# Leaving softmax probabilities undivided: inverse row sums moved into the output gates of both attention branches

## The chip, the cores and the metric

The kernel runs on one core of a Trainium2 chip. The core has a matrix engine (TensorE, PE in the profile), a vector engine (VectorE, DVE), a scalar engine (ScalarE, ACT), a general engine (GpSimd, POOL) and a queue that issues most transfers (SyncE, SP). The metric is the device time of one execution in microseconds (us); the median over the runs shown is what a change is judged by.

## The reference

Two layers of a Griffin-style block over 512 grid tokens (a grid of 8 rows by 64 columns) and 16 meta tokens, width 1024. Each layer makes one combined projection and splits it between grouped-query attention (branch A: 8 query heads, 2 key heads, head size 64) and neighbourhood attention on the grid (branch B: 8 heads, a clamped window of 8 by 16 neighbours and the meta keys). Each branch's output is multiplied by a SiLU gate, projected, merged by sigmoid gates and projected again.

```python
def attend(qb):                                   # branch A, also for the meta queries
    s = jnp.einsum('bqkgd,bskd->bkgqs', qb, k).astype(jnp.float32) * scale
    p = jax.nn.softmax(s, axis=-1).astype(v.dtype)
    return jnp.einsum('bkgqs,bskd->bqkgd', p, v)
...
# branch B, one grid row of queries
s = jnp.concatenate([s_win.reshape(b, NA_HEADS, GRID_W, kh * NA_KW), s_meta], axis=-1)
p = jax.nn.softmax(s, axis=-1).astype(v.dtype)
...
oa = gqa_attention(qa, ka, va) * jax.nn.silu(za)
ob = neighbourhood_attention(qb, kb, vb, rpb) * jax.nn.silu(zb)
ya = jnp.einsum('ble,ed->bld', oa, w_o_attn)
yb = jnp.einsum('ble,ed->bld', ob, w_o_na)
mixed = jax.nn.sigmoid(ga) * ya + jax.nn.sigmoid(gb) * yb
return x + jnp.einsum('bld,de->ble', mixed, w_out)
```

The inputs are drawn so that the scores are large (gains of the norms and of the bias table are scaled by about 8), so the row maximum is subtracted before the exponential.

## The kernel before, in words

**Layout.** Activations lie with features on the 128 partitions and the 528 tokens along the free axis, so a tile "512 or 528 wide" is one group of 128 features (a *pair* of heads, 64 partitions each) for all tokens. Everything is 32-bit. To keep accuracy, each operand of a big product is split into a rounded part (hi) and its remainder (lo) by `split` (L191: a cast on ACT at L193, a subtraction on DVE at L194), and a product is three matmuls (L325 to L327). Weights come in halves of 256 KB through four raw buffers; `weights` (L231) issues the load on SP (L235), casts on ACT (L240) and subtracts on POOL (L241), about one product ahead.

**Order of the work.** PE's backbone is the sequence of products: per layer 58 weight chunks, minus those of the last layer that are handled at the end. Each product covers the tokens in one span (second layer, 512 wide) or two (first layer, 264 wide each); 24 matmuls per span. After each span, and half way through a span of 512, `tick` (L310) lets the two attention branches emit one step. A unit of branch A starts every fourth tick and a head of branch B every fourth tick, one tick later; their further steps come a fixed number of ticks after their start, by the tables `GQA_AT` and `NA_AT` (L37 to L40). When the projections are over, `finish` (L299) lets the remaining ticks follow. What is emitted first has priority; a planner then orders each engine's instructions by priority and by the times that it expects, and the engines run their lists in that fixed order. `tc.high_priority()` lifts a piece; `tc.issue_after` holds one behind another on its engine.

**Branch A, one unit** (`global_unit`, L818; one head, two blocks of 128 queries, queries on partitions, 528 keys wide). `scores` at two ticks: `softmax` (L803) takes the scores from PSUM with the row maximum in one DVE operation (L810), negates the maximum (L813), applies the exponential on ACT with the row sum as a by-product (L814), then takes the inverse of the sum (L815) and multiplies the row by it (L816), both on DVE. `turn` (L833) transposes 32 by 32 blocks on DVE (L838) and, for the second block, writes the result to DRAM on SP (L841); `back` (L843) reads it so that keys lie on partitions (four transfers, L848, and a small one for the last keys, L851); `split_part` and `split_ends` make hi and lo parts (L193, L194, L867, L869); `sums` (L872) are the matmuls with the values (L876), in two groups of four and five. At the end `unit_done` (L903) adds the two halves of the result (`combine`, L765: a copy on ACT, an addition on DVE) into the pair's output tile; after the fourth unit of a pair `gated` (L775) multiplies that tile by the pair's gate on DVE (L777) and splits it. In the first layer there is also one unit per key head for the meta queries.

**Branch B, one head** (`windowed_head`, L931; four blocks of 128 queries against 208 or 272 keys). `prepare` loads the bias table; `scores` adds bias and takes the row extreme on DVE (L955), applies the exponential on ACT with row sums (L957), then inverts the sums (L953, L961, on DVE) and multiplies: two blocks on DVE (L960), two on ACT (L963). `transposes1` to `transposes3` turn the blocks on PE through two PSUM banks that they share with other small products and split them; `sums` multiplies with the values (L1022) and, for the second head of a pair, calls `gated` with the pair's gate `zb`. In the first layer the meta queries have their own small softmax (L971 to L974).

**Gates.** `silu_gate` (L752) makes `zb[j]` and `zgate[j]`, 128 partitions by 512 or 528 tokens, from the projections of pair j.

**The ends of the stages.** The products of branch B's output (WOB, written y<-ob in the profile) begin after the fourth of eight merge gates, which come behind the last pair's projection; those of branch A (WOA, y<-oa) follow in the same way behind a second set of eight merge gates. They take weight halves of four pieces, one piece per pair, so the last pair's gated tile is the fourth operand of the first of them.

The functions that the diff touches, with their callers:

Of the kernel before, what the change touches and what calls it, by code (L numbers as in the profile page):

```python
# [11 lines left out]
F32 = mybir.dt.float32  # L12
# [24 lines left out]
GQA_AT = ({"scores": (0, 2), "turn": (1, 3), "back": 4, "split": (5, 5), "ends": 5, "sums": (6, 7)},  # L37
          {"scores": (0, 1), "turn": (1, 2), "back": 3, "split": (5, 5), "ends": 5, "sums": (6, 7)})
# [57 lines left out]
def trunk_kernel(ctx: ExitStack, tc: tile.TileContext, xT, w, gn, gf, bias, rope, out):  # L96
# [357 lines left out]
    for l in range(DEPTH):  # L454
# [344 lines left out]


        zgate, oa, o_t, newest = {}, [None] * 4, {}, {}

        def softmax(p, q, qs, kv, k0, n, scale, name):  # L803
# [4 lines left out]
            with tc.high_priority():  # L808
# [5 lines left out]
                nc.scalar.activation(p[:n], p[:n], AF.Exp, bias=st[:n, 1:2], scale=1.0, accum_out=st[:n, 2:3])  # L814
            nc.vector.reciprocal(st[:n, 3:4], st[:n, 2:3])  # L815
            nc.vector.tensor_scalar_mul(p[:n], p[:n], st[:n, 3:4])  # L816

        def global_unit(kv, parts, n, name, done):  # L818
# [7 lines left out]
            def scores(i):  # L826
                q, qs, scale = parts[i]
# [3 lines left out]
                softmax(c["p"][i], q, qs, kv, NMETA - first_token[i], n, scale, f"{name}_{i}")  # L831
# [79 lines left out]
        def start_meta(kv):  # L911
            for j in (2 * kv, 2 * kv + 1):
                if j not in o_t:
                    o_t[j] = slot("T", f"oa{l}_{j}")
            return global_unit(kv, [(Q2m[kv], slice(0, 64), eighth)], 64, f"m{l}_{kv}", lambda av: meta_done(kv, av))

        def start_unit(hd, i):
            parts = [(Q2[hd], slice(P * t, P * (t + 1)), st["r8"][:, t, hd:hd + 1]) for t in (2 * i, 2 * i + 1)]
            return global_unit(hd // 4, parts, P, f"{l}_{hd}_{i}", lambda av: unit_done(hd, i, av))
# [11 lines left out]
        def windowed_head(hd):  # L931
# [9 lines left out]
            def scores():  # L941
                S = ps_s.tile([P, 2, 512], F32, tag="S", name=f"Sb{nm}")
                st = tiny.tile([P, 3, 4], F32, tag="stb", bufs=3, name=f"stb{nm}")
# [6 lines left out]
                for b, (base, k0, n) in enumerate(BLK):  # L950
                    i, c0 = BLK_PS[b]
                    if b == 2:
                        nc.vector.reciprocal(st[:, 2, :2], st[:, 1, :2])  # L953
                    with tc.high_priority():
                        nc.vector.tensor_tensor_reduce(pb[b], S[:, i, c0:c0 + n], pb[b], -1.0, 3e38,  # L955
                                                       ALU.add, ALU.min, st[:, 0, b:b + 1])
                    nc.scalar.activation(pb[b], pb[b], AF.Exp, bias=st[:, 0, b:b + 1], scale=-1.0,  # L957
                                         accum_out=st[:, 1, b:b + 1])
                for b in range(2):
                    nc.vector.tensor_scalar_mul(pb[b], pb[b], st[:, 2, b:b + 1])  # L960
# [320 lines left out]
```

## Time and profile before

| what | us |
|---|---|
| median of 3 runs (lowest, highest) | 867.78 (867.03, 868.68) |
| the profiled execution, its own time | 865.97 |
| its span, first to last instruction | 864.2 |
| time outside the span | 1.77 |
| PE busy in the span | 827.5 |
| DVE busy | 591.3 |
| ACT busy | 489.1 |
| POOL busy | 354.3 |

How to read it: "busy" counts an engine's instructions; an engine that waits for another is idle. Groups of instructions are named by the line of the kernel, the engine, the tile written, an arrow and the tiles read, followed by the shape, the count, and after a bar the busy time of the group, the mean duration of one in ns, and the idle time of the engine just before them with what ended it. "A <- B: t, n, longest" in the lists of waits says that instruction A of an engine waited for B, t us in total, n times. SPq stands for the queue of SP. DMA issues are listed with the KB of one and the median us from issue to landing. A table of windows gives, for a stretch of the span, the busy time of each engine and its instruction count.

### The profile page before, as it was taken

The page shows a single profiled execution, that of the slowest core. Times are in us where ns is not written, and L with a number is a line of the kernel's source. Part 1 is how long each engine was busy: PE and PEld are TensorE (multiplying, and loading weights), DVE is VectorE, ACT ScalarE, POOL GpSimd, SP SyncE. Part 2 cuts the span into 40 slices and gives each one's busy share as a digit, 9 for nine tenths or more (in the row PEclk, how much of TensorE's full clock was granted, in tenths as well). Part 3 has the DMA queues.
Part 4 walks back from the last instruction along what each step waited for, and adds up shares of the span by engine and source line. Part 5 has one row for each costly group of instructions (what it writes and reads, how often), then busy time and mean ns, then how long its engine had stood idle before and what let it go on. Part 6 is the DMA issues. An engine that isn't in the chain of part 4 may idle for free. (4 is left out here: it accounts for less than half of the span.)

```text
span 864.2 us, 16032 instructions
## 1 busy us (share of the span) xinstructions
PE 827.5 (96%) x5662; PEld 758.5 (88%) x5662; DVE 591.3 (68%) x1378; ACT 489.1 (57%) x1169; POOL 354.3 (41%) x279
## 2 busy tenths in 40 slices
PE   9999898989889999899999999999999899999997
PEld 9999898989889989799998989897888787878786
DVE  7987778878876685446456657677878767545633
ACT  8644676666765555334444547576768655443422
POOL 1653343422223333344675563333342333335751
PEclk9999999999999999999999999999999999999999
DMA  8366555636444555234655575656584454534502
GB/s 271 92 190 207 136 156 144 186 120 196 132 122 123 152 164 173 75 110 137 155 132 129 147 191 163 193 158 188 157 232 136 136 178 146 172 99 153 183 18 98
DMA packets 109664, 130.72 MB, mean 151 GB/s; under 512 B 30352, under 2 KB 64656, under 8 KB 109584
## 3 DMA queue, kind: packets, MB, share of 16 engines
q1 hardware_dynamic: 108864, 128.64, 50.7%
q8 instruction: 45, 0.74, 0.3%
q10 hardware_dynamic: 720, 1.06, 0.3%
q14 instruction: 35, 0.29, 0.1%
HBM read 94.30 MB, written 21.77 MB: 134 GB/s over the span
## 5 line engine op out<-in xcount | busy, mean ns | idle before, releaser
L241 POOL TENSOR_TENSOR wlo<-raw,whi 128x512 fp32r<-128x512 f32 x210 | 281.7, 1346 | 462.1 <-ACT whi L240 397.7
L325 PE MATMUL pp<-hh,whi 128*128 128x264 f32 (+3 forms) x1040 | 325.6, 313 | 0.3 <-DVE ma L1103 0.3
L327 PE MATMUL pp<-hh,wlo 128*128 128x264 f32 (+3 forms) x1040 | 325.1, 313 | 0.0
L326 PE MATMUL pp<-hl,whi 128*128 128x264 f32 (+3 forms) x1040 | 323.9, 311 | 0.0
L240 ACT CAST whi<-raw 128x512 fp32r<-128x512 f32 x210 | 129.0, 619 | 136.4 <-PE pp L326 43.3
L327 PEld LDWEIGHTS pp<-hh,wlo 128*128 128x128 f32 x1040 | 196.2, 189 | 10.5
L326 PEld LDWEIGHTS pp<-hl,whi 128*128 128x128 f32 x1040 | 196.6, 189 | 9.1
L325 PEld LDWEIGHTS pp<-hh,whi 128*128 128x128 f32 x1040 | 196.1, 189 | 9.1 <-DVE ma L1103 0.5
L194 DVE TENSOR_TENSOR ptl<-P,pth 128x512 fp32r<-128x512 f32 x64 | 52.7, 824 | 12.7 <-ACT pth L193 12.1
L810 DVE CUSTOM_DVE_ANT_1 P<-S,r 128x528 f32<-128x528 f32 x64 | 44.8, 699 | 9.6 <-PE S L557 8.6
L1097 DVE TENSOR_TENSOR mg<-pp,rbc 128x264 f32<-128x264 f32 (+1 forms) x48 | 24.5, 511 | 37.5 <-PE pp L327 37.3
L814 ACT ACTIVATE P<-P,st 128x528 f32<-128x528 f32 x64 | 47.2, 737 | 1.9
L838 DVE STREAM_TRANSPOSE P<-P 128x512 f32<-128x512 f32 x64 | 46.3, 724 | 1.3
L957 ACT ACTIVATE bias<-bias,stb 128x208 f32<-128x208 f32 (+1 forms) x64 | 31.0, 486 | 28.0 <-DVE stb L955 28.0
L876 PE MATMUL av<-ptl,VA 128*128 128x256 f32 x128 | 36.3, 305 | 6.2 <-DVE ptl L194 5.9
L876 PE MATMUL av<-pth,VA 128*128 128x256 f32 x128 | 37.3, 301 | 4.3 <-ACT pth L193 4.3
L193 ACT CAST pth<-P 128x512 fp32r<-128x512 f32 x64 | 39.3, 614 | 2.5 <-DMA P<-turn 1.5
L816 DVE TENSOR_SCALAR P<-P,st 128x528 f32<-128x528 f32 x64 | 37.1, 579 | 2.0
L1098 ACT ACTIVATE mg<-mg 128x264 f32<-128x264 f32 (+1 forms) x48 | 23.7, 493 | 23.8 <-DVE mg L1097 23.5
L326 PE MATMUL pp<-mx,whi 128*128 128x264 f32 x128 | 36.6, 286 | 0.0
L327 PE MATMUL pp<-mx,wlo 128*128 128x264 f32 x128 | 36.3, 284 | 0.0
L325 PE MATMUL pp<-mx,whi 128*128 128x264 f32 x128 | 36.3, 284 | 0.0
(533 smaller groups left out, 1739.5 us busy)
## 6 DMA issues: line engine op xcount, KB each, us to landing
raw<-in_w_dram SPq DMA_DIRECT2D x210, 256.0 KB, 2.9
turn<-P SPq DMA_DIRECT2D x32, 528.0 KB, 3.1
P<-turn SPq DMA_DIRECT2D x128, 128.0 KB, 3.1
bias<-in_bias_dram SPq DMA_DIRECT2D x16, 480.0 KB, 4.1
KB<-KB SPq DMA_DIRECT2D x24, 272.0 KB, 3.9
rawl<-in_w_dram SPq DMA_DIRECT2D x16, 256.0 KB, 3.1
x<-in_xT_dram SPq DMA_DIRECT2D x8, 264.0 KB, 4.9
xr<-in_xT_dram SPq DMA_DIRECT2D x8, 264.0 KB, 3.7
```

The lines of the kernel that those rows point to most:

```text
L193: split_at["hi"] = nc.scalar.copy(hi, src)
L194: split_at["any"] = nc.vector.tensor_sub(lo, src, hi.bitcast(F32))
L240: cast = nc.scalar.copy(hi, raw)
L241: sub = nc.gpsimd.tensor_sub(lo, raw, hi.bitcast(F32))
L325: nc.tensor.matmul(ps, wh, rh[:, a:b], start=i == 0, stop=False)
L326: nc.tensor.matmul(ps, wh, rl[:, a:b], start=False, stop=False)
L327: nc.tensor.matmul(ps, wl, rh[:, a:b], start=False, stop=i == n - 1)
L810: newest["max"] = nc.vector.tensor_tensor_reduce(p[:n].rearrange("p (i k) -> p i k", i=2), S[:n, :, :HALF], scale[:n].unsqueeze(2).to_broa ...
L814: nc.scalar.activation(p[:n], p[:n], AF.Exp, bias=st[:n, 1:2], scale=1.0, accum_out=st[:n, 2:3])
L816: nc.vector.tensor_scalar_mul(p[:n], p[:n], st[:n, 3:4])
L838: nc.vector.transpose(c["both"][:n, a:b], c["both"][:n, a:b])
L876: nc.tensor.matmul(c["av"], rows2(c["t"][i][0]), c["t"][i][1], start=i == 0, stop=i == 8)
```

## The change

Both branches stop dividing the probabilities of the real queries by their sums. The exponential writes each block's sums into one column of a small tile of 128 partitions by 8 that belongs to the pair (two heads by four blocks). A new function, `divided_later`, inverts the eight columns in one DVE operation, writes the 128 by 8 result to DRAM transposed (8 rows of 128), reads it back with two transfers that repeat each head's four rows over the 64 partitions of that head, into a tile from the pool G (8 buffers, shared with the splits of branch A and others), and multiplies the pair's gate by it on POOL. All three transfers are issued on SP. Branch A calls it at tick 3 of the pair's last unit; branch B in `transposes3` of the pair's second head. The two meta softmaxes (of branch A's meta unit and of branch B's meta queries) are divided as before. With it come new due times: in the first layer branch A's `scores`, `turn` and `back` move from ticks (0, 2), (1, 3), 4 to (0, 1), (1, 2), 3, as the second layer has them, and in both layers the two groups of `sums` move from ticks 6 and 7 to tick 7 both.

```diff
--- before.py
+++ after.py
@@ -34,8 +34,8 @@
 DEPTH = 2
 
 
-GQA_AT = ({"scores": (0, 2), "turn": (1, 3), "back": 4, "split": (5, 5), "ends": 5, "sums": (6, 7)},
-          {"scores": (0, 1), "turn": (1, 2), "back": 3, "split": (5, 5), "ends": 5, "sums": (6, 7)})
+GQA_AT = ({"scores": (0, 1), "turn": (1, 2), "back": 3, "split": (5, 5), "ends": 5, "divide": 3, "sums": (7, 7)},
+          {"scores": (0, 1), "turn": (1, 2), "back": 3, "split": (5, 5), "ends": 5, "divide": 3, "sums": (7, 7)})
 NA_AT = ({"stages": (0, 2, 5, 5, 5, 7), "values": (3, 4)},
          {"stages": (0, 2, 4, 5, 5, 7), "values": (3, 4)})
 
@@ -797,10 +797,24 @@
                     else:
                         nc.vector.scalar_tensor_tensor(to[low], tp[r], keep[r], to[r].bitcast(F32), op0=ALU.mult, op1=ALU.subtract)
 
-
-        zgate, oa, o_t, newest = {}, [None] * 4, {}, {}
-
-        def softmax(p, q, qs, kv, k0, n, scale, name):
+        def divided_later(sums, gate, name):
+
+            there = dpool.tile([8, P], F32, tag="sums", bufs=3, name=f"there{name}")
+            inverse = tiny.tile([P, 8], F32, tag="inverse", name=f"inv{name}")
+            nc.vector.reciprocal(inverse, sums)
+            nc.sync.dma_start(there.rearrange("g q -> q g"), inverse)
+            all_rows = slot("G", f"sums{name}")[:, :NREAL]
+            for hh in range(2):
+                r, _ = rows(hh)
+                nc.sync.dma_start(all_rows[r].rearrange("p (t q) -> p t q", t=4),
+                                  there[4 * hh:4 * hh + 4].unsqueeze(0).to_broadcast([HD, 4, P]))
+            nc.gpsimd.tensor_mul(gate[:, :NREAL], gate[:, :NREAL], all_rows)
+
+
+        zgate, oa, o_t, newest, sums_a = {}, [None] * 4, {}, {}, {}
+
+        def softmax(p, q, qs, kv, k0, n, scale, total, name):
+
             S = ps_s.tile([P, 2, 512], F32, tag="S", name=f"S{name}")
             for i in range(2):
                 score(S[:n, i, :HALF], q, KA2[kv], qs, slice(k0 + HALF * i, k0 + HALF * (i + 1)))
@@ -811,9 +825,11 @@
                     p[:n].rearrange("p (i k) -> p i k", i=2), S[:n, :, :HALF], scale[:n].unsqueeze(2).to_broadcast([n, 2, HALF]),
                     1.0, -3e38, ALU.mult, ALU.max, st[:n, 0:1])
                 nc.scalar.mul(st[:n, 1:2], st[:n, 0:1], -1.0)
-                nc.scalar.activation(p[:n], p[:n], AF.Exp, bias=st[:n, 1:2], scale=1.0, accum_out=st[:n, 2:3])
-            nc.vector.reciprocal(st[:n, 3:4], st[:n, 2:3])
-            nc.vector.tensor_scalar_mul(p[:n], p[:n], st[:n, 3:4])
+                nc.scalar.activation(p[:n], p[:n], AF.Exp, bias=st[:n, 1:2], scale=1.0,
+                                     accum_out=st[:n, 2:3] if total is None else total)
+            if total is None:
+                nc.vector.reciprocal(st[:n, 3:4], st[:n, 2:3])
+                nc.vector.tensor_scalar_mul(p[:n], p[:n], st[:n, 3:4])
 
         def global_unit(kv, parts, n, name, done):
 
@@ -824,11 +840,11 @@
             c = {"t": []}
 
             def scores(i):
-                q, qs, scale = parts[i]
+                q, qs, scale, total = parts[i]
                 if i == 0:
                     c["both"] = slots.tile([P, 2 * NTOK], F32, tag="M", bufs=BUFS["M"], name=f"P{name}")
                     c["p"] = [c["both"][:, NTOK * t:NTOK * (t + 1)] for t in range(len(parts))]
-                softmax(c["p"][i], q, qs, kv, NMETA - first_token[i], n, scale, f"{name}_{i}")
+                softmax(c["p"][i], q, qs, kv, NMETA - first_token[i], n, scale, total, f"{name}_{i}")
 
             def turn(i):
 
@@ -912,11 +928,18 @@
             for j in (2 * kv, 2 * kv + 1):
                 if j not in o_t:
                     o_t[j] = slot("T", f"oa{l}_{j}")
-            return global_unit(kv, [(Q2m[kv], slice(0, 64), eighth)], 64, f"m{l}_{kv}", lambda av: meta_done(kv, av))
+            return global_unit(kv, [(Q2m[kv], slice(0, 64), eighth, None)], 64, f"m{l}_{kv}", lambda av: meta_done(kv, av))
 
         def start_unit(hd, i):
-            parts = [(Q2[hd], slice(P * t, P * (t + 1)), st["r8"][:, t, hd:hd + 1]) for t in (2 * i, 2 * i + 1)]
-            return global_unit(hd // 4, parts, P, f"{l}_{hd}_{i}", lambda av: unit_done(hd, i, av))
+            j, g = hd // 2, 4 * (hd % 2) + 2 * i
+            if g == 0:
+                sums_a[j] = tiny.tile([P, 8], F32, tag="suma", name=f"suma{l}_{j}")
+            parts = [(Q2[hd], slice(P * t, P * (t + 1)), st["r8"][:, t, hd:hd + 1], sums_a[j][:, g + t - 2 * i:g + t - 2 * i + 1])
+                     for t in (2 * i, 2 * i + 1)]
+            steps = global_unit(hd // 4, parts, P, f"{l}_{hd}_{i}", lambda av: unit_done(hd, i, av))
+            if g == 6:
+                steps.append((GQA_AT[l]["divide"], lambda: divided_later(sums_a[j], zgate[j], f"a{l}_{j}")))
+            return sorted(steps, key=lambda x: x[0])
 
         for hd in range(8):
             if full and hd % 4 == 1:
@@ -940,7 +963,10 @@
 
             def scores():
                 S = ps_s.tile([P, 2, 512], F32, tag="S", name=f"Sb{nm}")
-                st = tiny.tile([P, 3, 4], F32, tag="stb", bufs=3, name=f"stb{nm}")
+                st = tiny.tile([P, 4], F32, tag="stb", bufs=3, name=f"stb{nm}")
+                if hh == 0:
+                    kvq[j]["sums"] = tiny.tile([P, 8], F32, tag="sumb", name=f"sumb{nm}")
+                total = kvq[j]["sums"][:, 4 * hh:4 * hh + 4]
 
                 pb = c["p"] = [c["bias"][:, base:base + n] for base, k0, n in BLK]
                 stacks["scored"] += 1
@@ -949,18 +975,11 @@
                     score(S[:, i, c0:c0 + n], c["q"], c["k"], slice(P * b, P * (b + 1)), slice(k0, k0 + n))
                 for b, (base, k0, n) in enumerate(BLK):
                     i, c0 = BLK_PS[b]
-                    if b == 2:
-                        nc.vector.reciprocal(st[:, 2, :2], st[:, 1, :2])
                     with tc.high_priority():
                         nc.vector.tensor_tensor_reduce(pb[b], S[:, i, c0:c0 + n], pb[b], -1.0, 3e38,
-                                                       ALU.add, ALU.min, st[:, 0, b:b + 1])
-                    nc.scalar.activation(pb[b], pb[b], AF.Exp, bias=st[:, 0, b:b + 1], scale=-1.0,
-                                         accum_out=st[:, 1, b:b + 1])
-                for b in range(2):
-                    nc.vector.tensor_scalar_mul(pb[b], pb[b], st[:, 2, b:b + 1])
-                nc.vector.reciprocal(st[:, 2, 2:], st[:, 1, 2:])
-                for b in range(2, 4):
-                    nc.scalar.mul(pb[b], pb[b], st[:, 2, b:b + 1])
+                                                       ALU.add, ALU.min, st[:, b:b + 1])
+                    nc.scalar.activation(pb[b], pb[b], AF.Exp, bias=st[:, b:b + 1], scale=-1.0,
+                                         accum_out=total[:, b:b + 1])
                 if full:
 
                     ps = bank(ps_t, f"sm{nm}", "tp")[:NMETA, :NMETA]
@@ -1002,6 +1021,8 @@
                 split(bh[:EDGE, 256:512], bl[:EDGE, 256:512], tp[:EDGE, 256:512])
 
             def transposes3():
+                if hh == 1:
+                    divided_later(kvq[j]["sums"], zb[j], f"b{l}_{j}")
                 tp = bank(ps_t, f"tc{nm}", "tp")
                 transposed(tp[:64, :P], c["bias"][:, BLK_META:BLK_META + 64])
 
```

## The prediction, made before the changed kernel was run

> **What bounds the kernel now.** I read the page first, then the busy time by stage, then PE's list of waits, then the timelines around the waits.
>
> ```profile
> span 864.2 us, 16032 instructions
> PE 827.5 (96%) x5662; PEld 758.5 (88%) x5662; DVE 591.3 (68%) x1378; ACT 489.1 (57%) x1169; POOL 354.3 (41%) x279
> ```
>
> PE is busy 827.5 of 864.2 us. The change touches no matmul, so all that it can win lies in PE's other 36.7 us. The windows (length, then busy time and count of PE, PE's weight loads, DVE, ACT, POOL; then clock and DMA) say where these lie: the two stretches in which the branches run beside the projections, the two in which the rest of branch A runs beside the merge, and the tail.
>
> ```profile
> 80.00:262.00 182.00, 168.61 (x1355) 163.76 (x1355) 147.32 (x412) 122.97 (x346) 57.92 (x47) 0.99 0.51 150
> 262.00:336.00 74.00, 70.96 (x564) 68.96 (x563) 53.45 (x125) 39.90 (x99) 25.63 (x19) 1.00 0.50 149
> 540.00:690.00 150.00, 142.51 (x879) 124.08 (x878) 116.66 (x309) 104.10 (x264) 51.71 (x40) 1.00 0.58 173
> 690.00:762.00 72.00, 70.69 (x343) 57.33 (x342) 49.00 (x97) 37.89 (x87) 27.08 (x22) 1.00 0.53 162
> 852.00:864.00 12.00, 6.34 (x51) 6.01 (x49) 4.77 (x12) 2.68 (x6) 1.22 (x2) 0.92 0.25 94
> ```
>
> PE idles 13.4, 3.0, 7.5 and 1.3 us in the first four, 25.2 us together; the tail's 5.7 us are outside the change. In the first DVE is busy 147.3 of 182 us (81%): with its own waits it is nearly full, and PE runs into it. PE's list of waits names the places:
>
> ```profile
> PE av L876 <- DVE ptl L194: 5.9, 14, 1.0
> PE av L876 <- ACT pth L193: 4.3, 6, 1.4
> PE tb L129 <- DVE tal L194: 4.0, 2, 2.3
> PE tc L129 <- DVE tal L194: 3.1, 2, 2.0
> PE y L325 <- ACT oa_3a L193: 2.7, 2, 2.2
> PE tb L129 <- DVE mm L990: 2.2, 1, 2.2
> PE av L876 <- DVE ga L869: 1.5, 3, 0.9
> ...
> PE tc L129 <- DVE mm L990: 1.1, 1, 1.1
> PE tm L129 <- DVE VB L194: 0.7, 1, 0.7
> PE ta L129 <- ACT bias L963: 0.6, 1, 0.6
> ```
>
> Three kinds: branch A's value matmuls waiting for their split operands, 5.9 + 4.3 + 1.5 = 11.7 us in many small pieces; branch B's small transposes on PE waiting for DVE to empty the bank that they need, 4.0 + 3.1 + 2.2 + 1.1 + 0.7 + 0.6 = 11.7 us in few large ones; the first product of branch A's output waiting for the last pair, 2.7 us.
>
> **The change: what it takes away.** These groups go (all 32 of L960 and L963, the 64 of L815 and L816), and one wait with them:
>
> ```profile
> L816 DVE TENSOR_SCALAR P<-P,st 128x528 f32<-128x528 f32 x64 | 37.1, 579 | 2.0
> L960 DVE TENSOR_SCALAR bias<-bias,stb 128x208 f32<-128x208 f32 (+1 forms) x32 | 10.6, 368 | 0.5
> L815 DVE RECIPROCAL st<-st 128x1 f32<-128x1 f32 x64 | 10.3, 162 | 37.9 <-ACT P L814 37.6
> L961 DVE RECIPROCAL stb<-stb 128x2 f32<-128x2 f32 x16 | 2.6, 162 | 1.4 <-ACT bias L957 1.3
> L953 DVE RECIPROCAL stb<-stb 128x2 f32<-128x2 f32 x16 | 2.5, 154 | 0.5
> L963 ACT ACTIVATE bias<-bias,stb 128x272 f32<-128x272 f32 (+1 forms) x32 | 14.2, 488 | 1.0 <-DVE stb L961 1.0
> L241 POOL TENSOR_TENSOR wlo<-raw,whi 128x512 fp32r<-128x512 f32 x210 | 281.7, 1346 | 462.1 <-ACT whi L240 397.7
> ```
>
> DVE loses 37.1 + 10.6 + 10.3 + 2.6 + 2.5 = 63.1 us of work, and 37.6 us in which it stood at L815 waiting for the exponential with other work queued behind it; ACT loses 14.2 us. It comes back as 16 inversions of 128 by 8 on DVE (at 0.16 us a row like L815's, 2.6 us). Spread over the 478 us of the four stages, DVE's 366.4 busy us fall by 60.5, so its share goes from 77% to 64%; the freed wait is worth nearly as much again to what is queued there. By itself none of this is time, since DVE and ACT are not the bound: it counts where PE waits.
>
> *Branch A's value matmuls.* The first four of nine move from tick 6 to tick 7, while their split stays at tick 5. One span of a product, the least that lies between two ticks, takes 3.0 us:
>
> ```profile
> 122.29 0.37 PE L325 MATMUL pp<-hh,whi 128*128 128x264 f32 x1
> 125.30 0.28 PE L1022 MATMUL avb<-na,VB 128*128 128x256 f32 x1
> ```
>
> The longest single wait is 1.4 us, so a wait at the first group is covered twice over. In the first layer the read-back also moves from tick 4 to 3, so that the split starts a tick after its data are asked for rather than close behind. What stays are waits at the second group and its end (ga). Bounds: 0 and 11.7 us; I take 9.
>
> *Branch B's transposes.* They wait for DVE in the crowded stages. With DVE's share down by a sixth and no stop at the exponential, I take a little under half of 11.7: 5 us. Bounds 0 (the waits are of order, not of load) and 11.7.
>
> *Branch A's last pair*, 2.7 us: its end is set by ACT's order (the cast of the last turned block stands behind weight casts). Earlier ticks help and the later first group hurts: 0, bounds −2 and +4.
>
> *The new due times in the first layer* put two score tiles on neighbouring ticks; both use one PSUM tile, which DVE frees in 0.7 us (L810's mean, 699 ns), under a tick: nothing, and at most a PE wait of that size per unit if DVE is late.
>
> **What it adds.** Per pair, 16 times: an inversion, a write of 4 KB in 1024 separate words, two reads of 128 KB, a POOL product of the size of L241's (1.35 us). Nearest rows for the transfers, and SP's own waits:
>
> ```profile
> x1d<-xt SPq DMA_DIRECT2D x32, 64.0 KB, 2.8
> pm<-turn SPq DMA_DIRECT2D x32, 16.0 KB, 2.6
> P<-turn SPq DMA_DIRECT2D x128, 128.0 KB, 3.1
> SPq L235 <- POOL wlo L241: 305.1, 141, 8.3
> SPq L848 <- DMA turn<-P: 38.0, 18, 3.8
> ```
>
> pm moves 128 runs of 128 bytes (32 rows by 4 blocks) in 2.6 us, x1d 512 such runs (32 by 16) in 2.8: four times the pieces cost 0.2 us, so 1024 words should take about 3.1; if the whole time went with the pieces it would be 5.6. I take 3.1, near the rows, and keep 5.6 as a rival. The chain from the sums to the finished gate is 0.16 + 3.1 + 3.1 + 1.35 = 7.7 us, with 2 us allowed for issues and hand-overs (an allowance, no row) some 10. The Trainium skill, page DMA: Bandwidth & Descriptors, section Rules for kernel authors, says that a strided last dimension lowers to one descriptor per element and should be rearranged; that speaks against this write. Its section Bandwidth gives about 10.5 ns per packet, which for 1024 words makes an estimated 10.8 us, a chain of 17.7 instead of 10, and by the pair with the least cover (below) a sum 6 to 7 us worse; no run here shows a transfer of single words.
>
> What covers the chain is the time between the last exponential of a pair and the multiplication by the gate. The two shortest that I found are those of the last pairs in the second layer, branch B first, then branch A:
>
> ```profile
> 673.72 0.19 ACT L957 ACTIVATION_READ_ACCUMULATOR bias<-bias,stb 128x1 f32 x1
> 685.16 0.69 DVE L777 TENSOR_TENSOR ob<-ob,zb 128x512 f32<-128x512 f32 x1
> 756.27 0.18 ACT L814 ACTIVATION_READ_ACCUMULATOR P<-P,st 128x1 f32 x1
> 774.68 0.69 DVE L777 TENSOR_TENSOR oa<-oa,za 128x512 f32<-128x512 f32 x1
> ```
>
> 685.16 − 673.91 = 11.3 us and 774.68 − 756.45 = 18.2 us. A chain of 10 fits, just, in the first.
>
> The second read waits on SP for the write to land, about 3 us per pair, 16 times 3 = 48 us in which SP issues nothing. Behind it stand weight loads, bias tables, turned blocks and the shifted halves of keys and queries. For the weights I cost it at nothing: SP already waits 305.1 us, 2.2 each, for a raw buffer to come free, so its loads run ahead. Turned blocks and shifted halves have no such lead; a delay of 3 us falls on a step that is due one tick later. On POOL the product stands ahead of weight subtractions that have 462.1 us of idle time before them. But POOL slows DVE:
>
> ```profile
> 188.76 1.35 DVE L194 TENSOR_TENSOR ptl<-P,pth 128x512 fp32r<-128x512 f32 x1 [1.63 <-ACT pth L193]
> 190.37 0.67 DVE L194 TENSOR_TENSOR ptl<-P,pth 128x512 fp32r<-128x512 f32 x1
> 188.29 1.28 POOL L241 TENSOR_TENSOR wlo<-raw,whi 128x512 fp32r<-128x512 f32 x1 [2.85 <-ACT whi L240]
> ```
>
> The same subtraction takes 1.35 us beside POOL and 0.67 alone, so 16 POOL products cost DVE up to 16 × 0.68 = 10.9 us, a sixth of what it gained. For all additions together I put 3 us on PE's path: bounds 0 and 16 (1 us per pair).
>
> **Sum.** −9 −5 + 0 + 3 = −11 us. The profiled execution took 865.97 us (span 864.2 and 1.77 around it), so 855.0 there; the median of the runs lies 1.8 above it, so 856.8: I forecast 857 us. The best ends give −11.7 −11.7 −2 = −25, 842; the worst ends of this mechanism 0 + 0 + 4 + 16, but these together are a case of their own, below.
>
> **The rivals.**
>
> *The waits move but do not shrink.* PE, arriving earlier, meets the next late operand, and what the first group of value matmuls no longer waits for the second group does. For it: 77% of DVE's load remains work in fixed order, and the large waits at the transposes may come from the planner's order alone. Against it: the waits are pieces of 0.3 to 2.3 us, and by the rows above a unit of branch A loses 2 × (0.58 + 0.16) = 1.5 us of DVE and a head of branch B 2 × 0.37 + 2 × 0.16 = 1.1 us, every fourth tick each. Then the gain is a few us and the 3 us of additions eat it: 866 to 869.5.
>
> *The gates come late (slower).* The write stands in SP's fixed order behind weight loads, each of which may wait up to 8.3 us for its buffer, and so does the read. With two waits of 2.2 the chain is 10 + 4.4 = 14.4, over the 11.3 us of one pair; with two of 8.3 it is 26.6, past the 18.2 as well. DVE then stands at L777 with PSUM evacuations behind it. PE has two PSUM buffers, so it goes on for about two spans, 6 us; the case decides from a lateness of 6 us, chains over 17 to 24 us. At 7.5 us late in all 16 pairs PE loses 1.5 each, 24 us: 867.8 − 14 + 24 = 878. Against it: the planner sees the sums early and SP waits for buffers most of the time, so it can put the write ahead.
>
> *The write is paid by the piece.* 5.6 us instead of 3.1, chain 12.5, late by 1.2 at one pair; SP's stops grow from 3.1 to 5.6 each, and in that proportion the 3 us of additions by 2.4: 857 + 1.2 + 2.4 = 861. The page of the Trainium skill named above holds the rule by which it would go so; its own price is given there.
>
> **How the numbers follow.** About 0.2% (1.7 us) is what a measurement of this kernel can tell from no change. The forecast's mechanism gets 0.66 (own range 848 to 864), the write paid by the piece 0.10, waits that move 0.10, late gates 0.14. So faster 0.76, same 0.10, slower 0.14. The range: 847 leaves out the last 4 or 5 us of the best bounds, 868 takes in most of the unchanged case; outside lie the late gates and a small part of the rest, about 0.2.
>
> **What would show it.** Right: PE's waits of av under 4 us together; those of tb, tc, tm and ta at 5 to 8; DVE busy near 535 us; no entry of DVE or ACT waiting at L777 for POOL; the write landing in 3 to 4 us; PE busy unchanged. Wrong: DVE idle before L777 by several us with POOL named; weight casts waiting for raw from DRAM; SP waiting long for the small write; or transposes still waiting 10 us although DVE is emptier.

## The result: 952.5 us, slower by 9.75%

The changed kernel takes 952.49 us (median of 4 runs, 948.76 to 956.52) where the kernel before takes 868.01 (867.03 to 868.68) beside it: a ratio of 1.0975, 95% interval 1.0921 to 1.1029. The forecast was 857, the range 847 to 868. The profiled execution took 954.97 us.

The page of the kernel after begins so:

```profile
span 953.0 us, 16027 instructions
PE 855.0 (90%) x5662; PEld 786.1 (82%) x5662; DVE 555.1 (58%) x1202; ACT 476.1 (50%) x1137; POOL 377.7 (40%) x295
PE 55%; DMA 21%; DVE 10%; ACT 6%; SPq 3%; issue 3%; POOL 1%; POOLq 0%; ACTq 0%; DVEq 0%
```

The work went as planned: PE has the same 5662 matmuls, DVE 176 instructions and 36 us less. Yet PE is idle for 953.0 − 855.0 = 98.0 us instead of 36.7, and its busy time for the same matmuls is 27.5 us longer. The third line is the chain that ended last, which now runs through DMA for 21% of the span. PE's list of waits, then that of all engines (engine, operand and line, what was waited for: us in total, times, longest):

```profile
PE av L892 <- ACT pth L193: 32.8, 6, 7.3
PE y L325 <- ACT ob L193: 10.0, 1, 10.0
PE tb L129 <- DVE tal L194: 9.7, 3, 8.5
PE av L892 <- DVE ptl L194: 7.1, 11, 1.1
```

```profile
DVE ptl L194 <- ACT pth L193: 56.2, 18, 8.4
ACT pth L193 <- DMA P<-turn: 45.4, 9, 9.6
ACT whi L240 <- DMA raw<-in_w_dram: 44.8, 10, 9.8
```

Before, PE waited in pieces of at most 2.3 us; now six waits for ACT's split of a turned block cost it 32.8. ACT in turn waits for transfers: for turned blocks 45.4 us and for raw weights 44.8, up to 9.8 at a time. The change alters neither transfer (in the first layer it only asks for the turned blocks a tick earlier). The queue of SP and one pair's surroundings (first SP's list of waits, then its timeline, then those of ACT, POOL, DVE and PE at the same place):

```profile
SPq L809 <- DMA thereb<-invb: 49.6, 7, 8.6
SPq L809 <- DMA therea<-inva: 47.2, 8, 8.3
```

```profile
736.47 0.38 SPq L805 DMA_DIRECT2D thereb<-invb  x1
736.94 2.54 SPq L864 DMA_DIRECT2D P<-turn  x4
739.52 0.60 SPq L867 DMA_DIRECT2D pm<-turn  x1
747.04 1.12 SPq L809 DMA_DIRECT2D sumsb<-thereb  x2
```

```profile
751.94 0.62 ACT L193 CAST pth<-P 128x512 fp32r<-128x512 f32 x1 [9.57 <-DMA P<-turn]
```

```profile
753.16 1.26 POOL L811 TENSOR_TENSOR zb<-zb,sumsb 128x512 f32<-128x512 f32 x1 [9.42 <-DMA sumsb<-thereb]
```

```profile
757.36 0.69 DVE L777 TENSOR_TENSOR ob<-ob,zb 128x512 f32<-128x512 f32 x1
```

```profile
758.76 0.79 PE L325 MATMUL y<-ob,whi 128*128 128x512 f32 x1 [9.98 <-ACT ob L193]
```

The write goes out at 736.47, the read that waits for it at 747.04. In between only the four reads of turned blocks and the small one for the last keys (pm) are issued, and before the change a read of a turned block landed after 3.1 us; ACT is still waiting for them at 751.94, behind it DVE, and PE stands for 10 us. The gate was not what it waited for: POOL had it ready at 754.42, and DVE came to it at 757.36, straight from the late splits (no idle time stands beside its row). In the whole trace DVE's L777 waits for POOL once, 3.4 us. What the DMA engines did meanwhile shows the DMA view of 735 to 755, 40 slices of 0.5 us:

```profile
DMA  9986479942932122816334217634999879899410
GB/s 406 304 262 254 86 222 217 92 62 34 35 28 14 19 42 24 38 19 43 16 28 24 23 40 24 13 42 103 263 297 259 168 278 387 324 385 385 156 41 16
```

From 739 to 748.5, nineteen slices, they move 13 to 62 GB/s with half a megabyte of turned blocks asked for; before the words of the write go out it is 254 to 406, and from 749 to 753.5 it is 168 to 387. The words of the write are through by then: the trace's packet records have nearly all of them between 737.5 and 739. So the question for the experiments was what the 4 KB do to everything behind them.

### The profile page after: what moved, and what is told of

The parts are those of the page before. It is cut to its first block, busy times and chain, and to the rows that moved or that the text cites. A ratio compares the mean times of both kernels' runs of the same rounds, so it can differ in the third digit from the quotient of the medians.

```text
span 953.0 us, 16027 instructions
## 1 busy us (share of the span) xinstructions
PE 855.0 (90%) x5662; PEld 786.1 (82%) x5662; DVE 555.1 (58%) x1202; ACT 476.1 (50%) x1137; POOL 377.7 (40%) x295
## 4 chain that ended last, share of the span: by engine, by line
PE 55%; DMA 21%; DVE 10%; ACT 6%; SPq 3%; issue 3%; POOL 1%; POOLq 0%; ACTq 0%; DVEq 0%
PE pp L327 12%; PE pp L325 12%; PE pp L326 12%; DMA P<-turn 8%; DMA turn<-P 3%; DMA raw<-in_w_dram 3%; PE av L892 3%; DVE ptl L194 2%; PE y L325 2%; PE y L326 2%; PE y L327 2%; DMA thereb<-invb 2%; SPq L864 2%; DVE ga L885 2%; PE pf L1221 1%
## 5 line engine op out<-in xcount | busy, mean ns | idle before, releaser
L325 PE MATMUL pp<-hh,whi 128*128 128x264 f32 (+3 forms) x1040 | 334.4, 322 | 3.4 <-ACT whi L240 1.8
L327 PE MATMUL pp<-hh,wlo 128*128 128x264 f32 (+3 forms) x1040 | 333.5, 321 | 0.7 <-POOL wlo L241 0.7
L326 PE MATMUL pp<-hl,whi 128*128 128x264 f32 (+3 forms) x1040 | 332.4, 320 | 0.0
L240 ACT CAST whi<-raw 128x512 fp32r<-128x512 f32 x210 | 128.6, 618 | 178.1 <-DMA raw<-in_w_dram 44.8
L325 PEld LDWEIGHTS pp<-hh,whi 128*128 128x128 f32 x1040 | 203.9, 196 | 13.6 <-ACT whi L240 2.0
L327 PEld LDWEIGHTS pp<-hh,wlo 128*128 128x128 f32 x1040 | 203.8, 196 | 12.5 <-POOL wlo L241 1.2
L326 PEld LDWEIGHTS pp<-hl,whi 128*128 128x128 f32 x1040 | 204.5, 197 | 9.8
L194 DVE TENSOR_TENSOR ptl<-P,pth 128x512 fp32r<-128x512 f32 x64 | 57.3, 897 | 67.2 <-ACT pth L193 56.2
L892 PE MATMUL av<-pth,VA 128*128 128x256 f32 x128 | 38.4, 321 | 32.8 <-ACT pth L193 32.8
L193 ACT CAST pth<-P 128x512 fp32r<-128x512 f32 x64 | 39.1, 613 | 45.5 <-DMA P<-turn 45.4
L824 DVE CUSTOM_DVE_ANT_1 P<-S,r 128x528 f32<-128x528 f32 x64 | 44.8, 701 | 21.2 <-PE S L557 20.6
L892 PEld LDWEIGHTS av<-pth,VA 128*128 128x128 f32 x128 | 27.2, 213 | 34.8 <-ACT pth L193 34.4
L325 PE MATMUL y<-ob,whi 128*128 128x264 f32 (+1 forms) x96 | 31.2, 325 | 10.0 <-ACT ob L193 10.0
L892 PEld LDWEIGHTS av<-ptl,VA 128*128 128x128 f32 x128 | 27.0, 211 | 11.6 <-DVE ptl L194 11.0
```

The lines of the kernel that those rows point to most:

```text
L193: split_at["hi"] = nc.scalar.copy(hi, src)
L194: split_at["any"] = nc.vector.tensor_sub(lo, src, hi.bitcast(F32))
L240: cast = nc.scalar.copy(hi, raw)
L325: nc.tensor.matmul(ps, wh, rh[:, a:b], start=i == 0, stop=False)
L326: nc.tensor.matmul(ps, wh, rl[:, a:b], start=False, stop=False)
L327: nc.tensor.matmul(ps, wl, rh[:, a:b], start=False, stop=i == n - 1)
```

## The experiments

Times are medians, each beside runs of the kernel before on the same chip (866.9 to 868.3 us). First the change was taken apart.

**No division at all.** The body of `divided_later` is left out.

```diff
         def divided_later(sums, gate, name):
-            there = dpool.tile([8, P], F32, tag="sums", bufs=3, name=f"there{name}")
...
-            nc.gpsimd.tensor_mul(gate[:, :NREAL], gate[:, :NREAL], all_rows)
+            pass
```

> The changed kernel without divided_later: no inversion, no transfers, no product on POOL, so the output is not divided by the sums; everything else, the due times too, as changed. Theory R (ring): the write of 1024 single words occupies the DMA engines for about 8 to 10 us per pair (in the changed kernel one was issued at 164.84 and the read behind it at 175.37) and everything issued behind it lands late. Theory Q (queue): SP loses the time because the read stands in its fixed order waiting for the write (49.6 + 47.2 us of waits). Theory T (times): the new due times and the new order cost the time. R and Q both expect 850 to 862 here, the gain that the prediction summed without its additions (868.0 - 14 = 854). T expects over 920.

Measured: 844.63 us, ratio 0.9727 (0.9699 to 0.9755): −22.3 us, more than expected. From its page and PE's list of waits:

```profile
PE 821.5 (97%) x5662; PEld 760.1 (90%) x5662; DVE 541.3 (64%) x1186; ACT 476.8 (57%) x1137; POOL 357.2 (42%) x279
```

```profile
PE tb L129 <- DVE mm L1000: 3.8, 2, 3.1
PE av L883 <- DVE ga L876: 2.1, 3, 0.9
PE av L883 <- DVE ptl L194: 1.8, 4, 0.7
PE tb L129 <- DVE tal L194: 1.7, 3, 0.7
PE tc L129 <- DVE tal L194: 1.4, 1, 1.4
...
PE y L325 <- ACT oa_3a L193: 1.0, 1, 1.0
```

Branch A's value matmuls wait 3.9 us instead of 11.7, branch B's small transposes 6.9 instead of 11.7, the last pair 1.0 instead of 2.7. PE's busy time falls by another 6.0. So the loss is all in what the change adds. The 6.0 are not less work: the durations of all matmul records add up to 1740.3 us before and 1740.1 here. The busy time counts records that overlap once, and here they overlap more.

**The new due times alone**, in the kernel before:

```diff
-GQA_AT = ({"scores": (0, 2), "turn": (1, 3), "back": 4, "split": (5, 5), "ends": 5, "sums": (6, 7)},
-          {"scores": (0, 1), "turn": (1, 2), "back": 3, "split": (5, 5), "ends": 5, "sums": (6, 7)})
+GQA_AT = ({"scores": (0, 1), "turn": (1, 2), "back": 3, "split": (5, 5), "ends": 5, "sums": (7, 7)},
+          {"scores": (0, 1), "turn": (1, 2), "back": 3, "split": (5, 5), "ends": 5, "sums": (7, 7)})
```

> The kernel before with the new due times of branch A alone; divisions as they were. The run without division gained 22 us with both. By the prediction's first term 9 us come from the due times: 857 to 860. If they come from the removed divisions (DVE emptier), the due times alone give 865 to 870.

Measured: 868.06 us, ratio 1.0007 (0.9996 to 1.0019): nothing. PE's list of waits says why:

```profile
PE tb L129 <- DVE mm L990: 7.3, 2, 4.3
PE tb L129 <- DVE tal L194: 4.9, 6, 1.4
PE av L876 <- DVE ga L869: 3.7, 5, 0.9
PE av L876 <- DVE ptl L194: 2.9, 7, 0.7
PE tm L129 <- DVE VB L194: 2.3, 2, 1.3
PE tc L129 <- DVE tal L194: 2.2, 2, 2.0
```

The value matmuls' waits do shrink, from 11.7 to 6.6 us, but those of tb, tm and tc grow from 11.1 to 16.7 in these rows: with DVE as full as before the wait only moves to the other branch. The gain needs the divisions gone.

**The write in runs of 32 bytes**, as the sums lie in SBUF:

```diff
-            there = dpool.tile([8, P], F32, tag="sums", bufs=3, name=f"there{name}")
+            there = dpool.tile([P, 8], F32, tag="sums", bufs=3, name=f"there{name}")
...
-            nc.sync.dma_start(there.rearrange("g q -> q g"), inverse)
+            nc.sync.dma_start(there, inverse)
...
-                                  there[4 * hh:4 * hh + 4].unsqueeze(0).to_broadcast([HD, 4, P]))
+                                  there[64 * hh:64 * hh + 64].rearrange("(t a) b -> t (a b)", t=4).unsqueeze(0).to_broadcast([HD, 4, P]))
```

> The changed kernel with the inverse written as it lies, 128 rows of 8 words, and read back as 64 copies of 512 words in a row: the same bytes, the same waits, the same reads and product, but 128 pieces of 32 bytes in place of 1024 of 4. The transposition is left out, so the factors stand at the wrong queries. R: the write lands in about 3 us, the waits for the read fall from 7 to about 3 us, the time is 855 to 872. Q: the read still stands behind the write, so about 3/7 of the loss of 84 us stays: 890 to 905. T: over 920.

Measured: 857.95 us, ratio 0.9874 (0.9833 to 0.9915). The same bytes, the reads still waiting for the write, the same POOL products: 94.5 us less than the change. The write lands as fast as theory R expected, and the turned blocks as fast as before:

```profile
thereb<-invb SPq DMA_DIRECT2D x8, 4.0 KB, 2.2
P<-turn SPq DMA_DIRECT2D x128, 128.0 KB, 3.2
```

**The write unread.** It stays in 1024 words, but the reads fetch another tile, filled once, so nothing on SP waits for the write to land.

```diff
+            if l == 0:
+                fixed = dpool.tile([8, P], F32, name="fixed")
+                nc.sync.dma_start(fixed.rearrange("g q -> q g"), eighth.to_broadcast([P, 8]))
...
-                                  there[4 * hh:4 * hh + 4].unsqueeze(0).to_broadcast([HD, 4, P]))
+                                  fixed[4 * hh:4 * hh + 4].unsqueeze(0).to_broadcast([HD, 4, P]))
```

> The changed kernel with the write of 1024 words kept as it is, but the two reads take their rows from another DRAM tile that is filled with 0.125 once at the start, so SP never stands at a read for the write; the gates get 0.125 in place of the inverse sums. R: the turned blocks and weights issued behind a write still land 8 us late, PE still waits for the split operands: over 910. Q: the loss is gone, 855 to 870. T: over 920.

Measured: 926.47 us (two runs), ratio 1.0672 (1.0627 to 1.0716). SP's wait for the write is worth 26 us; most of the loss comes without it. Nine turned blocks that were asked for within 9 us after a write have a landing in the trace, 11.6 us in the median.

```profile
thereb<-invb SPq DMA_DIRECT2D x8, 4.0 KB, 10.8
therea<-inva SPq DMA_DIRECT2D x8, 4.0 KB, 11.2
```

Here is the price of the write: 10.8 to 11.2 us (medians of the six landings that the trace gives, 9.1 to 13.4), where the prediction had 3.1 and at most 5.6. The Trainium skill, page DMA: Bandwidth & Descriptors, section Bandwidth, with its 10.5 ns per packet gave the estimate of 10.8: the number agrees, though the page states the figure for loads issued by GpSimd. Whether its reason does was the next question.

**The same write in the kernel before, unread**, from a constant tile:

```diff
+        def unread(name, n=8):
+            there = dpool.tile([n, P], F32, tag="sums", bufs=3, name=f"there{name}")
+            nc.sync.dma_start(there.rearrange("g q -> q g"), ident[:, :n])
```

> The kernel before, divisions and due times as they were, with nothing added but the write: 16 times, at the places where the changed kernel issues it, 1024 words go from a constant tile to a DRAM tile that nobody reads. Nothing waits for the write itself. Theory R (the write holds the DMA engines for about 10 us and what stands behind it on SP's queue lands late): 915 to 940, that is most of the 68.5 us by which the run with the unread write (926.5) lay over the run with 128 short runs (858.0), and PE waiting for value operands, turned blocks and weights. Rival S (late transfers hurt only because the new due times put the split one tick behind the read-back and left no slack): under 885, since the old times leave a tick more.

Measured: 917.25 us, ratio 1.058 (1.0559 to 1.0601). The number lies in the expected range of the ring theory, but the run doesn't bear it out: with nothing to wait for, all 16 writes were issued between 13.6 and 73.6 us, and the loss is two waits of PE there, not one at each pair.

```profile
PE pp L325 <- ACT ks L492: 21.4, 1, 21.4
PE mt L637 <- ACT msb L631: 20.9, 1, 20.9
```

It shows only that such writes hurt without the rest of the change. SP's own issues slowed too: this one takes 7.68 us, where the write at 736.47 above took 0.38 (its timeline):

```profile
49.98 7.68 SPq L803 DMA_DIRECT2D therea<-ident  x1
```

**The write on ACT's queue**, the reads on SP as before:

```diff
-            nc.sync.dma_start(there.rearrange("g q -> q g"), inverse)
+            nc.scalar.dma_start(there.rearrange("g q -> q g"), inverse)
```

> The changed kernel with the write of 1024 words issued on ACT's queue instead of SP's; the two reads stay on SP and still wait for it. Theory RQ (the harm is order within SP's queue: what stands behind the write waits until its words are through): transfers behind it on SP go round it, turned blocks land in 3 to 4 us again, but the read's wait on SP stays at about 8 us and holds SP up: 868 to 900. Rival RE (the harm is in the DMA engines, which every queue shares): turned blocks still land in 8 to 12 us and the time is 935 to 955.

Measured: 949.98 us, ratio 1.0968 (1.0924 to 1.1012), as slow as the change. Five turned blocks that were asked for behind a write have a landing here, 12.1 us in the median: rival RE. Order within SP's queue is not the cause. The Trainium skill, page DMA: Bandwidth & Descriptors, section Rules for kernel authors, says that transfers issued from several engines share the same 16 DMA engines, so that spreading them gains no bandwidth; this run agrees (949.98 against 952.49). The DMA view of 778 to 798 (40 slices of 0.5 us; the write is issued at 779.26) shows more than sharing:

```profile
DMA  0000999699935695345746315864156999999999
GB/s 0 0 0 8 363 422 287 5 327 242 20 12 33 53 37 25 16 29 29 37 29 29 19 9 31 41 34 27 17 59 136 267 293 264 276 255 258 226 352 442
```

From 783 to 793 the engines are busy, mostly a third to nine tenths of the time, and move 9 to 59 GB/s: they hold packets that are slow to finish. In the packet records half of the 2 KB packets of the run take 0.08 us, and many take 0.5 to 2.7 us here. That points behind the engines, to where the words go.

**The words apart in DRAM.** As the unread write, but with unused bytes between the words. This is the run with 64 bytes from word to word; the next has 512 (a last dimension of 128).

```diff
-            there = dpool.tile([8, P], F32, tag="sums", bufs=3, name=f"there{name}")
+            there = dpool.tile([8, P, 16], F32, tag="sums", bufs=3, name=f"there{name}")
...
-            nc.sync.dma_start(there.rearrange("g q -> q g"), inverse)
+            nc.sync.dma_start(there.rearrange("g q s -> q g s")[:, :, 0:1], inverse.unsqueeze(2))
```

> As the run with the unread write (reads from a tile filled once, so the output isn't divided by the right sums), but the 1024 words of a write go 64 bytes apart in DRAM, over 64 KB, instead of side by side in 4 KB. In the traces the words themselves have passed the engines 2 us after the issue; then packets of 2 KB that took 0.12 us take 0.5 to 2.7 us for some 8 us. Theory L (words side by side in one short stretch of memory are taken in one after another, and all else that goes there waits): 860 to 885, write landing in under 5 us. Rival W (each word written to DRAM costs its 10 ns wherever it goes) and rival R (the engines' work with 1024 pieces): 915 to 935, landing in 10 us as before.

> The same with the words 512 bytes apart, over 512 KB. L: 855 to 885, like 64 bytes or better, if the stretch that words share is up to 512 bytes long. W and R: 915 to 935.

Measured: 853.83 us, ratio 0.9831 (0.9811 to 0.9852), and 853.37, ratio 0.9827 (0.979 to 0.9863). 1024 pieces of 4 bytes to DRAM as before, and 72.6 us less than side by side (926.5 − 853.8), below even what theory L expected. The DMA view with 64 bytes:

```profile
P<-turn SPq DMA_DIRECT2D x128, 128.0 KB, 3.5
thereb<-invb SPq DMA_DIRECT2D x8, 4.0 KB, 3.4
therea<-inva SPq DMA_DIRECT2D x8, 4.0 KB, 4.5
```

So the price is neither the engines' for the pieces nor one per word written: the words hinder each other, and others, when they lie close together in DRAM. The Trainium skill's figure met the number by chance; as a price per packet it would have given 10.8 here too.

**The words into SBUF**, in eight partitions and eight DMAs:

```diff
+            there = slot("G", f"there{name}")[:8, :P]
...
+            for g in range(8):
+                nc.sync.dma_start(there[g:g + 1], inverse[:, g:g + 1])
```

> As the run with the unread write, but the 1024 words go into eight partitions of SBUF instead of DRAM, in eight DMAs of 128 words. The number and the size of pieces stay. W and L (the price is DRAM's for small writes): 860 to 885, landing in under 5 us, the eight issues costing SP 2 to 3 us per pair. R (the price is the engines' for the pieces): 915 to 940.

Measured: 885.43 us, ratio 1.0196 (1.0176 to 1.0217), just over the range of the DRAM theories and 41 below the same words side by side in DRAM. Each of the eight lands in 2.0 us, and PE's longest group of waits is for something else, POOL's part of the weights. The 16 × 8 issues take SP's time (in the timeline four of them take 3.56 us), but ACT's weight casts wait for raw weights only 2.7 us, so why POOL is late stays open:

```profile
thereb<-invb SPq DMA_DIRECT2D x64, 0.5 KB, 2.0
```

```profile
PE pp L327 <- POOL wlo L241: 9.3, 9, 2.1
```

It speaks against the engines as the cause, less cleanly than the runs before.

**How close is close.** 16 and 32 bytes from word to word (last dimension 4 and 8), and 16 bytes in the order of the partitions, so that four neighbours come from one partition:

```diff
+            there = dpool.tile([P, 8, 4], F32, tag="sums", bufs=3, name=f"there{name}")
...
+            nc.sync.dma_start(there[:, :, 0:1], inverse.unsqueeze(2))
```

> As the run with words 64 bytes apart (853.8, reads from a tile filled once), in the same transposed order, but 16 bytes apart, four words to 64 bytes. If words hinder each other that fall in the same 64 bytes, some of the 73 us come back: 865 to 905; if the stretch is 16 bytes or shorter: 850 to 858.

> The same, 32 bytes apart, two words to 64 bytes. With a stretch of 64 bytes: between the run with 16 bytes and 854, 856 to 880; with a stretch of 32 bytes or less: 850 to 858.

> Words 16 bytes apart as in the run before the last, but in the order of the partitions, so that the four words of 64 bytes come from one partition, one behind the other in one engine. If the hindrance comes from several engines writing into one stretch at a time: 850 to 860 and below the transposed order at the same distance. If any two words in one stretch hinder each other: the same time as the transposed order, within 5 us.

Measured: 856.60 us (ratio 0.9861, 0.9835 to 0.9888) with 16 bytes, 853.01 (0.9833, 0.9804 to 0.9862) with 32, 870.95 (1.0039, 1.002 to 1.0058) with 16 in the order of the partitions. The write to the gates of branch B lands so, first 16 bytes transposed, then 32, then 16 by partitions:

```profile
thereb<-invb SPq DMA_DIRECT2D x8, 4.0 KB, 3.8
```

```profile
thereb<-invb SPq DMA_DIRECT2D x8, 4.0 KB, 3.5
```

```profile
thereb<-invb SPq DMA_DIRECT2D x8, 4.0 KB, 5.4
```

From 16 bytes on nearly all is regained, so a stretch of 64 bytes, which four words would share, is not the rule; and neighbours from one partition are worse by 14 us, not better, which neither expectation had. That speaks against my guess that several engines writing at one place do the harm. Which property of the memory it is, if it is the memory's, stays open: between 4 and 16 bytes nothing was tried, and the write's extent (4 to 512 KB) grew with the distance.

**The idea done well.** First by rows: PE turns the 128 by 8 inverses (one small transposition per pair), DVE empties the bank, and the write is 8 runs of 512 bytes.

```diff
+            ps = bank(ps_t, f"is{name}", "tp")
+            nc.tensor.transpose(ps[:8, :P], inverses[name], ident)
...
+            eight = slot("G", f"eight{name}")
+            nc.vector.tensor_copy(eight[:8, :P], ps[:8, :P])
+            nc.sync.dma_start(there, eight[:8, :P])
```

> The changed kernel with the inverse sums turned on PE first (one transposition of 128 by 8 per pair, emptied by DVE), so that the write to DRAM is 8 runs of 512 bytes; the reads and the product on POOL stay. If the price of the change lies in the single words and nowhere else, this keeps the change's idea and costs what the run with 128 runs of 32 bytes cost, 858, give or take 4 for 16 small transpositions and copies: 852 to 862, write landing in about 2 us. If it is the way through DRAM as such that costs (a write, a wait and two reads), it stays over 868.

Measured: 864.18 us, ratio 0.9952 (0.9929 to 0.9974): 0.5% faster than before, but above the expected 852 to 862. PE now meets other late products of DVE; the largest are `mg`, the gate of the merge, and a split:

```profile
PE y L325 <- DVE mg L1130: 4.6, 2, 3.5
PE av L901 <- DVE ptl L194: 4.3, 7, 1.0
PE tb L129 <- DVE mm L1021: 4.1, 2, 3.2
```

The same with the product on DVE (`nc.vector.tensor_mul` in place of `nc.gpsimd.tensor_mul`):

> The kernel with the inverses turned on PE and written as 8 rows (864), with the product of gate and inverse sums on DVE instead of POOL. If POOL's 22 us of products, which slow DVE, are what keeps it 10 us above the kernel with four PE transpositions (853): 852 to 858. If it is the reads and SP's waits: 862 to 870.

Measured: 862.63 us, ratio 0.9937 (0.9915 to 0.9959). POOL's products are not what keeps it there. The time lies where the reads and SP's waits were expected to hold it, but no run takes these apart.

Then without DRAM: ACT spreads the inverses over 128 by 512, four transpositions on PE bring them to the gate's partitions, DVE multiplies the gate by PSUM.

```diff
+            nc.scalar.copy(f.rearrange("p (t h d) -> p t h d", t=4, h=2),
+                           inverse.rearrange("p (h t) -> p t h", h=2).unsqueeze(3).to_broadcast([P, 4, 2, HD]))
...
+            for t in range(4):
+                nc.tensor.transpose(ps[:, P * t:P * (t + 1)], wide[name][:, P * t:P * (t + 1)], ident)
+            nc.vector.tensor_mul(gate[:, :NREAL], gate[:, :NREAL], ps)
```

> No transfer at all: the inverse is spread by one copy on ACT to 128 by 512 (0.6 us), turned by four transposes on PE into a PSUM bank (0.6 us), and DVE multiplies the gate by the bank (0.7 us); the full computation. PE gains 16 x 0.5 us of work against the version without any division, ACT 10 us, DVE 11 us. R and Q: 858 to 868, between the version without division plus 8 us and the kernel before. T: over 920.

Measured: 853.32 us, ratio 0.9829 (0.9802 to 0.9855): 1.7% faster than the kernel before, and the fastest here that leaves nothing out. It keeps 866.94 − 853.32 = 13.6 of the 22.3 us. Most of the rest is probably its 64 transpositions (5726 − 5662), for PE's busy time is 6.8 us above that without division:

```profile
PE 828.3 (97%) x5726; PEld 764.7 (90%) x5726; DVE 552.7 (65%) x1218; ACT 485.7 (57%) x1153; POOL 356.3 (42%) x279
```

## Why the prediction was wrong

The runs add up from one kernel to the next: before 866.9; without division 844.6 (−22.3); with inversions, reads, products and a write whose words lie apart 853.8 (+9.2); words side by side 926.5 (+72.6); reads that wait for that write 952.5 (+26.0).

- *Branch A's value matmuls, −9*: right as a sum, −7.8. The reason was half right: the due times alone shift 5 us of it to branch B.
- *Branch B's transposes, −5*: right, −4.8. *The last pair, 0*: −1.7, within its bounds.
- *PE's busy time unchanged*: wrong by −6.0 us without division, though the matmuls' own durations add up to the same; closer overlap is a gain that the sum of waits had no term for. Together with the idle time (36.7 to 842.9 − 821.5 = 21.4) this makes the gain 22 instead of 14.
- *DVE near 535 us*: 541.3 without any addition. The groups that went took 63.1 us, the total fell by 50.0. Of the other 13, 8.3 came back in branch A's small subtraction `ga` (64 of them, 23.8 to 32.1 us, a mean of 372 to 502 ns).
- *Additions, +3 (0 to 16)*: 9.2 with the words 64 bytes apart and unread, 858.0 − 844.6 = 13.3 with the write in runs of 32 bytes that the reads wait for: in the bounds, but three to four times the 3. That this last kernel takes 858, a microsecond above the forecast of 857, is luck: the gain was larger by 8 us and the additions by 10.
- *The write, 3.1 us, at most 5.6*: this is the step that failed. "Four times the pieces cost 0.2 us, so 1024 words should take about 3.1" carried rows with runs of 128 bytes over to words side by side. Its two rows aren't even of one kind: pm is read from DRAM, x1d is written to it. The price is not by the piece: the same 1024 pieces take 3.4 to 4.5 us with 64 bytes from word to word and 10.8 to 11.2 side by side. Even the upper end was half the truth.
- *Who pays for it*: the second failure, and the dearer. The prediction counted the landing against the gate's cover and SP's standing (48 us expected, 49.6 + 47.2 measured). It held no place for the write slowing transfers that don't depend on it: "for the weights I cost it at nothing" became ACT waiting 44.8 us for raw weights, and the turned blocks, a delay of 3 us put at one tick, came about 10 late. 72.6 of the 107.9 us of additions have this cause.
- *The rivals*: "the gates come late" had the right side and the wrong place. Its sign, DVE idle before L777 for POOL, is one wait of 3.4 us. The other three signs named for a wrong forecast all came: weight casts waiting for raw from DRAM (44.8 us), SP waiting long for the small write (49.6 and 47.2) and transposes still waiting 10 us (PE's tb for tal, 9.7) although DVE is emptier. *The write is paid by the piece* had the longer write in view, but as a price of the write itself, 861 in all, and not as a harm to other transfers.

## What to carry to other kernels

Don't write single words side by side into DRAM, as a transposition by access pattern does: turn the data on PE or write whole runs, and if single words can't be avoided leave room between them (32 bytes from word to word cost no more here than 512; 16 depended on the order). Price a transfer by rows of its own shape; where the trace has none, an extrapolation from longer runs is no upper bound. And ask of a new transfer not only when it lands and who waits for it, but what else is in flight at that time.

## What the runs showed of the hardware that was not expected

A write of 4 KB in single words side by side can hold up other transfers for about 9 us, those of another queue too (the run with the write on ACT's queue). The engines' busy share is then still 0.43, by the last two columns of the first row below, and they move 33 GB/s; with a share of 0.60, in the second row, they move 179. Read the two together: busy engines alone would pass for a load.

A long stall of PE is paid twice. The view by windows of the kernel after, 10 us before, in and after the stall at 748.8 (start and end, length, PE, PE's weight loads, DVE, ACT, POOL, granted clock, DMA share, GB/s):

```profile
738.50:748.50 10.00, 9.67 (x49) 7.63 (x48) 2.86 (x7) 2.50 (x7) 1.28 (x1) 1.00 0.43 33
748.50:758.50 10.00, 0.28 (x2) 0.00 (x0) 5.63 (x7) 3.24 (x7) 2.73 (x2) 0.72 0.60 179
758.50:768.50 10.00, 9.68 (x39) 7.86 (x40) 4.70 (x10) 4.33 (x11) 2.58 (x2) 0.77 0.29 91
```

The granted clock is 0.72 on average while PE stands, and 0.77 over the 10 us after it, in which PE is as busy as before the stall. In windows of 1 us it is 1.00 until 752, 0.50 from 753 to 763 and 1.00 again from 764: it falls about 4 us after PE stopped at 748.8 and comes back about 4 us after PE went on at 758.8. Over the run PE's busy time for the same matmuls grows by 27.5 us, so nearly a third of the 88.8 us by which the span grew isn't idle time. The Trainium skill, page TensorE: Matmul & The Clock Gate, section Part 1: The HAM clock gate, says that the clock is halved after an idle window of about 3.4 us and comes back after a busy one; these windows agree.
